# Rotating images by 90 degrees: stores no longer held until the loads have landed, and a last load in half rows

## The chip, the cores and the metric

The kernel runs on one core of one Trainium2 chip. The metric is device time in microseconds (us) of that core; lower is better. Several executions are timed without a profile, and one more is profiled.

## The reference

```python
batch, c, h, w = 32, 3, 256, 256
x = np.random.randn(batch, c, h, w).astype(np.float32)
out = np.rot90(x, k=-1, axes=(-2, -1)).astype(np.float32)
```

Each of 96 images of 256 by 256 float32 values is turned clockwise by 90 degrees: `out[b, c, i, j] = x[b, c, 255 - j, i]`. No arithmetic is done. 25.17 MB are read and 25.17 MB written.

## The kernel before

All 96 images fit into SBUF at once. They are taken as five groups `u0` to `u4` of 2, 2, 2, 4 and 2 slabs (`sizes`, line 38); a slab is 2 MB, 16 KB in each of 128 partitions. A group has a tile of its own, which is loaded, turned in place and stored, so no buffer is used twice.

**Loads.** All loads are issued by the sync engine (SP), in program order. Group 0 comes by two transfers of 1 MB (line 55) and one of 2 MB (line 56), in pieces of 8 KB. For the other groups there are as many transfers as slabs (line 66), of 2 MB each, and each writes every second partition, or every fourth in group 3 (`to[i::I]`): groups 1, 2 and 4 in pieces of 16 KB over 64 partitions, group 3 in pieces of 32 KB over 32 partitions. The very last 2 MB, slab 1 of group 4, are split in two: line 63 loads the first half `a = 0` of the group's images and line 64 the second half `a = 1`, 1 MB each, 64 pieces of 16 KB. There are fourteen loads.

**Turning.** VectorE (DVE) transposes blocks of 32 by 32. Group 0 is done by `turn_slab` (line 72), the others by `turn_group`: one quarter (or two instructions for group 3) goes into a held tile, `extra` or the PSUM tiles `spare` (line 88), the other three are turned inside the group's tile (line 93), and then ScalarE (ACT) copies the held quarter into its place (lines 78 and 98). VectorE and ScalarE follow program order, group after group.

**Stores.** Ten stores (lines 106 and 113) are issued by the sync engine as well, after all loads in program order: two for each group, each from every second partition, in pieces of 16 KB over 64 partitions. They are 2 MB each, 4 MB for group 3. A store waits until VectorE and ScalarE have finished its group. The first store also waits until the transfer of line 63, called `mark`, has landed, by a dependency put in by hand (lines 107 to 109). Since the sync engine works through its instructions in order, this holds all later stores too.

**Semaphores.** The framework gives DMA transfers eight completion semaphores in turn. The ninth transfer therefore waits on the sync engine until the first has landed, the tenth until the second has, and so on; this is what spaces the later loads.

Of the kernel before, what the change touches and what calls it, by code (L numbers as in the profile page):

```python
# [1 line left out]

# [4 lines left out]


@with_exitstack  # L10
def kernel(
    ctx: ExitStack,
    tc: tile.TileContext,
    x: bass.AP,
    out: bass.AP,
):

    nc = tc.nc
    fp32 = mybir.dt.float32

    B, C, H, W = x.shape
    P = nc.NUM_PARTITIONS
    R = 16  # L30
    E = R * W
    hw = R // 2
    low, high = slice(0, hw), slice(hw, R)

    rows_in = x.rearrange("b c h w -> (b c h) w")
    rows_out = out.rearrange("b c h w -> (b c h) w")

    sizes = (2, 2, 2, 4, 2)
    first = [sum(sizes[:n]) for n in range(len(sizes))]
    groups = [  # L40
        ctx.enter_context(tc.tile_pool(name=f"group{n}", bufs=1)).tile([P, s, E], fp32, name=f"u{n}")
        for n, s in enumerate(sizes)
    ]
    psum = ctx.enter_context(tc.tile_pool(name="psum", bufs=1, space=bass.MemoryType.PSUM))
    spare = [psum.tile([P, E // 2], fp32, name=f"spare{h}") for h in range(2)]
    extra = ctx.enter_context(tc.tile_pool(name="extra", bufs=1)).tile([P, E // 2], fp32, name="extra")

    def rows_of(rows, n):
        return rows[first[n] * P * R : (first[n] + sizes[n]) * P * R]


    ld = rows_of(rows_in, 0).rearrange("(s i p r) w -> s i p (r w)", s=2, i=2, p=P)
    home = [groups[0][:, s].rearrange("p (i f) -> p i f", i=2) for s in range(2)]
    for i in range(2):
        nc.sync.dma_start(out=home[0][:, i], in_=ld[1, i])  # L55
    nc.sync.dma_start(out=home[1], in_=ld[0].transpose([1, 0, 2]))
    for n in range(1, len(sizes)):
        I = sizes[n]
        ld = rows_of(rows_in, n).rearrange("(a i m r) w -> i m a (r w)", a=2, i=I, m=P // I)
        to = groups[n].rearrange("p s f -> p (s f)").rearrange("p (a f) -> p a f", a=2)  # L60
        for i in range(I):
            if (n, i) == (len(sizes) - 1, I - 1):
                mark = nc.sync.dma_start(out=to[i::I, 0], in_=ld[i][:, 0])
                nc.sync.dma_start(out=to[i::I, 1], in_=ld[i][:, 1])
            else:
                nc.sync.dma_start(out=to[i::I], in_=ld[i])

    def turn_slab(src, dsts):
        s = src.rearrange("p (i r g c) -> p c r g i", i=2, r=R // 2, c=R)
        for h, d in enumerate(dsts):  # L70
            d = d.rearrange("p (c k r) -> p c r k", c=hw, r=R // 2)[:, :, ::-1, ::-1]
            nc.vector.transpose(out=d, in_=s[:, h * hw : (h + 1) * hw])  # L72

    u = groups[0]
    turn_slab(u[:, 0], spare)
    turn_slab(u[:, 1], [u[:, 0, : E // 2], u[:, 0, E // 2 :]])
    for h in range(2):
        nc.scalar.copy(out=u[:, 1, h * E // 2 : (h + 1) * E // 2], in_=spare[h])  # L78

    def turn_group(n, held):  # L80
        I = sizes[n]
        T = I // 2
        K = W // (R * T)
        u = groups[n].rearrange("p s f -> p (s f)")
        src = u.rearrange("p (a t r g c) -> p t c r g a", a=2, t=T, r=R, c=R)
        dst = u.rearrange("p (i c k t r) -> p t c r k i", i=I, c=R, k=K, t=T)[:, ::-1, :, ::-1, ::-1, :]
        for t in range(T):
            nc.vector.transpose(  # L88
                out=held[t].rearrange("p (i c k r) -> p c r k i", i=I, c=hw, k=K)[:, :, ::-1, ::-1, :],
                in_=src[:, t, low, low])  # L90
        for c, r in ((low, high), (high, high), (high, low)):
            for t in range(T):
                nc.vector.transpose(out=dst[:, t, c, r], in_=src[:, t, c, r])  # L93
        back = u.rearrange("p (i c k t r) -> p t i c k r", i=I, c=R, k=K, t=T)[:, ::-1]
        for t in range(T):
            kept = held[t].rearrange("p (i c k r) -> p i c k r", i=I, c=hw, k=K)
            for i in range(I):
                nc.scalar.copy(out=back[:, t, i, low, :, high], in_=kept[:, i])  # L98

    for n, held in enumerate(([extra], [spare[1]], spare, [extra]), 1):  # L100
        turn_group(n, held)


    st = rows_of(rows_out, 0).rearrange("(s i m r) w -> i m s (r w)", s=2, i=2, m=P // 2)
    for a in range(2):
        put = nc.sync.dma_start(out=st[a], in_=groups[0][a::2])
        if a == 0:
            tc.add_manual_dep(put.ins, mark.ins.name, mybir.DependencyInfo(
                mybir.DependencyClass.Sync, mybir.DependencyReason.SCHED_ONLY), reason="stores after loads")
    for n in range(1, len(sizes)):  # L110
        st = rows_of(rows_out, n).rearrange("(a i m r) w -> a m i (r w)", a=2, i=sizes[n], m=P // 2)
        for a in range(2):
            nc.sync.dma_start(out=st[a], in_=groups[n][a::2])


# [1 line left out]
_INS = ['x']  # L117
_OUTS = [((32, 3, 256, 256), 'float32')]


# [23 lines left out]
```

## Time and profile before

| | |
|---|---|
| median of 3 runs | 122.95 us (122.94 to 122.95) |
| the profiled execution | 122.88 us |
| its span, first to last instruction | 121.1 us |
| VectorE busy | 87.4 us, 24 instructions |
| ScalarE busy | 14.9 us, 17 instructions |
| DMA, mean over the span | 416 GB/s |
| DMA packets | 3456 (384 of them under 512 B) |
| hold of the first store on the sync engine (line 106) | 31.2 us |

The page gives the busy share of the engines in forty slices of the span, and for the DMA engines the mean over the core's sixteen. "SPq" stands for the sync engine's instruction queue: an issue there is the moment when a transfer is handed to the DMA queue, not when its bytes move. The time from an issue to the landing includes the time that the transfer stands behind others. In the view of windows, a DMA share is summed from the packets that end in a window, so that it can lie a little above 1 in a short one. GB/s counts loads and stores together.

### The profile page before, as it was taken

What the parts mean: (1) busy time and instruction counts of PE and PEld (TensorE: products, weight loads), DVE (VectorE), ACT (ScalarE), POOL (GpSimd) and SP (SyncE); (2) the same over time, 40 slices, a digit from 0 to 9 for tenths busy, and PEclk for the clock granted to TensorE, in tenths of its full rate; (3) what the DMA queues carried; (4) which work ended last, traced back from release to release, by engine and by line L of the source; (5) the groups of instructions that cost most, each with busy time, mean ns of one, the idle gap of its engine ahead of it and who ended that gap; (6) DMA issues with size and microseconds to landing.
All of it is one profiled execution on the core that took longest, in us unless ns stands there. A gap on an engine that the chain in (4) does not pass through costs nothing.

```text
span 121.1 us, 131 instructions
## 1 busy us (share of the span) xinstructions
DVE 87.4 (72%) x24; ACT 14.9 (12%) x17; POOL 0.2 (0%) x4
## 2 busy tenths in 40 slices
DVE  0039999999999999999999999999999600000000
ACT  0000400380005100060000000318000330000000
POOL 0000000000000000000000000000000000000000
DMA  2999999999989898999999999999999999999994
GB/s 89 428 428 422 452 433 433 433 433 433 520 346 520 346 520 346 428 422 411 433 433 428 433 433 428 417 417 433 428 433 433 433 433 433 433 433 433 433 422 184
DMA packets 3456, 50.33 MB, mean 416 GB/s; under 512 B 384, under 2 KB 384, under 8 KB 384
## 3 DMA queue, kind: packets, MB, share of 16 engines
q1 hardware_dynamic: 3456, 50.33, 97.6%
HBM read 25.17 MB, written 25.17 MB: 416 GB/s over the span
## 4 chain that ended last, share of the span: by engine, by line
DVE 66%; issue 6%; DMA 6%; ACT 1%; ACTq 1%; SPq 0%; DVEq 0%
DVE u L93 39%; DVE spare L88 9%; DVE extra L88 6%; DVE u L72 6%; DVE spare L72 6%; DMA u<-in_x_dram 6%; ACT u L98 1%; ACTq L139 1%; SPq L55 0%; DVEq L88 0%; DVEq L72 0%
## 5 line engine op out<-in xcount | busy, mean ns | idle before, releaser
L93 DVE STREAM_TRANSPOSE u<-u 128x2048 f32<-128x2048 f32 x15 | 54.4, 3649 | 0.4
L72 DVE STREAM_TRANSPOSE spare<-u 128x2048 f32<-128x2048 f32 x2 | 7.1, 3586 | 8.1 <-DMA u<-in_x_dram 8.1
L98 ACT COPY u<-spare 128x512 f32<-128x512 f32 (+1 forms) x10 | 6.0, 687 | 38.5 <-DVE u L93 38.5
L88 DVE STREAM_TRANSPOSE spare<-u 128x2048 f32<-128x2048 f32 x3 | 10.7, 3588 | 0.0
L72 DVE STREAM_TRANSPOSE u<-u 128x2048 f32<-128x2048 f32 x2 | 7.8, 3988 | 0.0
L88 DVE STREAM_TRANSPOSE extra<-u 128x2048 f32<-128x2048 f32 x2 | 7.8, 3896 | 0.0
L98 ACT COPY u<-extra 128x1024 f32<-128x1024 f32 x4 | 4.0, 1043 | 22.8 <-DVE u L93 22.8
L78 ACT COPY u<-spare 128x2048 f32<-128x2048 f32 x2 | 3.6, 1870 | 8.7 <-DVE u L72 8.7
L78 ACT ACT_TABLE_LOAD x1 | 1.3, 1283 | 13.0 <-DMA u<-in_x_dram 13.0
L128 POOL MEMSET const-uint8-127<- 128x1 uint8 x1 | 0.1, 103 | 0.0
L128 POOL MEMSET const-bfloat16-1.0<- 128x1 bf16 x1 | 0.1, 102 | 0.0
L128 POOL MEMSET const-float32-0.0<- 128x1 f32 x1 | 0.1, 99 | 0.2 <-issue 0.2
L128 POOL MEMSET const-float32-1.0<- 128x1 f32 x1 | 0.1, 99 | 0.0
## 6 DMA issues: line engine op xcount, KB each, us to landing
u<-in_x_dram SPq DMA_DIRECT2D x10, 2048.0 KB, 30.4
out_dram<-u SPq DMA_DIRECT2D x8, 2048.0 KB, 18.2
out_dram<-u SPq DMA_DIRECT2D x2, 4096.0 KB, 21.1
u<-in_x_dram SPq DMA_DIRECT2D x4, 1024.0 KB, 20.5
```

The costliest lines, as they stand in the source:

```text
L72: nc.vector.transpose(out=d, in_=s[:, h * hw : (h + 1) * hw])
L78: nc.scalar.copy(out=u[:, 1, h * E // 2 : (h + 1) * E // 2], in_=spare[h])
L88: nc.vector.transpose(out=held[t].rearrange("p (i c k r) -> p c r k i", i=I, c=hw, k=K)[:, :, ::-1, ::-1, :], in_=src[:, t, low, low])
L93: nc.vector.transpose(out=dst[:, t, c, r], in_=src[:, t, c, r])
L98: nc.scalar.copy(out=back[:, t, i, low, :, high], in_=kept[:, i])
L128: nc = _bacc.Bacc("TRN2", target_bir_lowering=False, num_devices=1)
L139: with _tile.TileContext(nc) as tc:
```

## The change

The dependency of the first store on the transfer `mark` goes, so a store waits only for its own group (and for the turn of its semaphore). The last 2 MB are still loaded by two transfers of 1 MB, but cut in another way: each now brings one half `f` of every row of 16 KB, for both halves `a` of the group, so 128 pieces of 8 KB over the same 64 partitions two apart. Line numbers after line 109 move up by three.

```diff
             if (n, i) == (len(sizes) - 1, I - 1):
-                mark = nc.sync.dma_start(out=to[i::I, 0], in_=ld[i][:, 0])
-                nc.sync.dma_start(out=to[i::I, 1], in_=ld[i][:, 1])
+                for f in (slice(0, E // 2), slice(E // 2, E)):
+                    nc.sync.dma_start(out=to[i::I, :, f], in_=ld[i][:, :, f])
             else:
                 nc.sync.dma_start(out=to[i::I], in_=ld[i])
...
     for a in range(2):
-        put = nc.sync.dma_start(out=st[a], in_=groups[0][a::2])
-        if a == 0:
-            tc.add_manual_dep(put.ins, mark.ins.name, mybir.DependencyInfo(
-                mybir.DependencyClass.Sync, mybir.DependencyReason.SCHED_ONLY), reason="stores after loads")
+        nc.sync.dma_start(out=st[a], in_=groups[0][a::2])
```

## The prediction

> **What bounds the kernel now.** I began with the page: busy shares, the forty slices, the queues.
>
> ```profile
> DVE 87.4 (72%) x24; ACT 14.9 (12%) x17; POOL 0.2 (0%) x4
> ...
> DMA  2999999999989898999999999999999999999994
> ...
> q1 hardware_dynamic: 3456, 50.33, 97.6%
> ```
>
> VectorE works 87.4 us of 121.1. The DMA engines are full from the first slice to the last, and all 50.33 MB of loads and stores pass through one queue, q1. The chain of waits ends on VectorE and ScalarE at about 97 us, because it does not follow the last stores; I read it only as the order in which groups become ready. What sets the end is that queue. The question is therefore whether the transfers ever stand still, above all where loads end and stores begin. Next I read the timeline of the sync engine's issues, in the stretches 7 to 9, 12 to 14, 15 to 35 and around 59 us (start, duration, line, count):
>
> ```profile
> 7.98 0.60 SPq L66 DMA_DIRECT2D u<-in_x_dram  x1
> ...
> 12.95 0.60 SPq L66 DMA_DIRECT2D u<-in_x_dram  x1
> ...
> 17.84 0.61 SPq L66 DMA_DIRECT2D u<-in_x_dram  x1
> 22.75 0.51 SPq L63 DMA_DIRECT2D u<-in_x_dram  x1
> 27.64 0.49 SPq L64 DMA_DIRECT2D u<-in_x_dram  x1
> ...
> 59.43 1.37 SPq L106 DMA_DIRECT2D out_dram<-u  x2
> 60.92 39.06 SPq L113 DMA_DIRECT2D out_dram<-u  x8
> ```
>
> Each of the first five waits for an earlier load to land, so these starts are landings: the second transfer of group 0 at 7.98, its third (2 MB) at 12.95, then both of group 1 and the first of group 2. Loads land in the order of issue, one 2 MB after the other. The last load (L64) is in the queue from 27.64 on. The first store goes in at 59.43, and the view of the sync engine's waits says what it stood for:
>
> ```profile
> SPq L106 <- DMA u<-in_x_dram: 31.2, 1, 31.2
> ```
>
> That 31.2 us is the hold which the change removes. It looks large, so I asked for the windows around it, one for each 0.61 us (start and end, length, VectorE, ScalarE and GpSimd busy, clock, DMA share, GB/s):
>
> ```profile
> 59.84:60.45 0.61, 0.61 (x1) 0.00 (x0) 0.00 (x0) 1.00 1.01 430
> 60.45:61.06 0.61, 0.61 (x1) 0.00 (x0) 0.00 (x0) 1.00 1.01 430
> 61.06:61.67 0.61, 0.61 (x1) 0.00 (x0) 0.00 (x0) 1.00 1.01 430
> 61.67:62.28 0.61, 0.61 (x1) 0.00 (x0) 0.00 (x0) 1.00 1.00 430
> ```
>
> The transfers pass from loads to stores at 430 GB/s without a dip. The hold is a wait of the sync engine, not of the DMA engines.
>
> **The hold.** Removed: one semaphore wait of the first store, on L63's landing. The order of the sync engine's instructions in the changed kernel is otherwise the same: fourteen loads first, ten stores after, no load behind a store. What the first store then waits for is ScalarE's last copy of group 0 (23.03 + 3.63 = 26.7 us) and the landing of an earlier transfer that used its semaphore, the second of group 2. Landings go on from 27.64 in steps of 4.9, so that is 32.5 us. The others follow: the second store at about 37.4, group 1 at 42.3 and 47.2, group 2 at 54.2 (its copies end at 52.19 + 1.93 = 54.1) and 57.1; groups 3 and 4 as before, at 84.25 and 97.94, when their copies are done. But at 32.5 us all loads are already queued, 28 us of them, and the stores stand behind. Gain: only what is lost at the seam now. L64 was issued at 27.64 and took 34.1 us to land, 61.74; the first store was issued at 59.43 and took 7.2, 66.6. The difference is 4.9 us for 2 MB, as much as one load behind another. I take 0 for the seam, and 0.1 us (the rounding of the landing times) as the most there is to gain.
>
> That the stores stay behind the loads is the row on which all rests: from 5.6 us on some eight transfers stood in one queue at once, and every landing that the trace shows came in the order of issue. The Trainium skill ("DMA: Bandwidth & Descriptors", section "Queues, rings and completion order") says that an engine takes descriptors of one ring in order, but alternates by packets between rings of different queue rows. By its first half the removal is worth nothing; by its second, with stores on another queue than the loads, it would start the sharing that I price below as a rival.
>
> **The half rows.** Before, L63 and L64 bring 64 pieces of 16 KB each, over 64 partitions two apart; after, 128 pieces of 8 KB each, over the same partitions. That is 128 pieces more, 8 more for each of 16 engines. Same bytes, same number of transfers and of issues (L63 and L64 take 0.51 and 0.49 us on the sync engine, hidden by a queue that is 30 us ahead). The nearest row is group 0's third transfer, 2 MB in 8 KB pieces: 12.95 - 7.98 = 4.97 us. 2 MB in 16 KB pieces took 17.84 - 12.95 = 4.89, 22.75 - 17.84 = 4.91 and 27.64 - 22.75 = 4.89, on average 4.90. So half rows cost 0.07 us for the last 2 MB, and since the queue never empties, all of it goes to the end. The far row is the start: the first 2 MB in such pieces land at 7.98, though the windows show bytes from 2.3 on, 5.7 us, 0.8 more than 4.90, filling of the pipe included. That is the upper bound. Below nothing I leave 0.02, the scatter of the three steps. I take 0.07, since the third transfer stands in a full queue as these do.
>
> The same page of the skill, in "Why small descriptors are slow", puts a fixed overhead of about 3 bus cycles on a packet; 8 x 3 cycles at 850 MHz would make an estimate of 0.03 us, and the sum 122.91 on the profiled execution.
>
> **What it moves.** Group 4 is complete 0.07 us later, at 61.8 instead of 61.74, but VectorE turns to it at 81.04: hidden by 19 us. Group 3, which VectorE takes up at 52.12 just after it has landed (issued at 12.95, 39.1 us to landing: 52.05), lies ahead of the changed transfers and is not touched. The engines meet the same waits. Group 3's store is issued at 84.25; the windows show the last bytes near 119.4, and groups 3 and 4 are 12.58 MB, at 4.90 us for 2.097 MB 29.4 us; so without group 3 the queue runs dry at 90.0. A store's first bytes came 1.6 us after its issue at the start (0.73 to 2.35), so it may be issued as late as 88.4: cover 4.1 us.
>
> **Sum.** Seam 0, half rows +0.07. On the profiled execution, 122.88 us (span 121.1 and 1.78 around it), that gives 122.95. The median of the runs is 122.95, 0.07 above that execution, so the forecast is 123.02: +0.06%, where about 0.2% (0.25 us) is what a measurement of this kernel can tell from no change.
>
> **Rivals.**
>
> Stores share the engines with the loads (slower). If a store issued at 32.5 us advanced beside the loads, packet for packet, group 3's loads (19.5 us of them left then) would land up to 19.5 us later, as each landing admits another store. VectorE waits for them from 52.1 on, and group 3's store comes at 84.25 + 19.5 = 103.8. All other work in the queue would end at 90.0, so the engines would idle for 19.5 - 4.1 = 15.4 us: 138.4. It decides from a delay of group 3 above 4.1 us; a single 2 MB store overtaking (4.9 us) costs 0.8, 123.8. For it speaks that VectorE has no slack at 52.12; against it, that one queue has landed everything in order. Chance 0.09.
>
> Half rows of 8 KB two apart are dearer than the contiguous 8 KB pieces of group 0 (slower). No transfer of before reads 8 KB and leaves out the next 8 KB. Toward the bound of 0.8 that gives 123.2 to 123.75. Against it: loads of 16 KB pieces one MB apart and 32 KB pieces keep the same rate. Chance 0.13.
>
> The seam hides a stall (faster). The hold releases the first store at 59.43, only 2.3 us before the loads have landed, and one engine might wait for its store although the sum over sixteen shows no dip. Early issue would return at most 0.1 by the landings, 122.92 with the half rows counted, which is no measurable change; to pass 0.2% it needs over 0.3 us (122.7), which no row shows. Chance 0.08, half of it for a real gain.
>
> The change does nothing: the hold is removed, yet the stores still start when the loads are done. That is part of my forecast.
>
> **How the numbers follow.** The forecast has 0.68, the three rivals 0.09, 0.13 and 0.08, and 0.02 are left for a gain that I do not see. Unchanged: 0.68 and half of the seam case, 0.72. Slower by over 0.2%: 0.09 + 0.13 = 0.22. Faster: the other half of the seam case and the rest, 0.06. The range goes from 122.8 (122.95, less 0.1 for the seam and 0.02 for the pieces) to 123.8 (the far bound of the half rows, and a single store that overtakes); sharing beyond one store and a real gain are left out, less than 0.15. Its likeliest part is 122.85 to 123.1.
>
> **What would show it.** Right: 3584 packets instead of 3456; stores of group 0 issued near 32.5 and 37.4 us but landing 66 us or later; L64's second transfer landing near 61.8; 430 GB/s through 61 us; VectorE still at 52.1 for group 3; the last bytes near 119.4. Wrong: a store that lands before 61 us, an idle VectorE at 52 us, or steps of the last two load landings above 2.6 us each.

## The result: 0.3% slower, and the profile after

The changed kernel takes 123.38 us (median of 6 runs, 123.25 to 123.51) where the kernel before took 122.94 beside it: a ratio of 1.0033, 95% interval 1.002 to 1.0046. That is 0.44 us, little, but clear of the scatter. The profiled execution took 123.42 us, its span 121.6.

The page's lines that were shown of before read now:

```profile
DVE 87.4 (72%) x24; ACT 14.9 (12%) x17; POOL 0.2 (0%) x4
...
DMA  3999999999979898999999999999999999999993
...
DMA packets 3584, 50.33 MB, mean 414 GB/s; under 512 B 384, under 2 KB 384, under 8 KB 384
...
q1 hardware_dynamic: 3584, 50.33, 97.5%
```

The 128 pieces more are there. VectorE and ScalarE do what they did, and the queue still looks full. The timeline of the sync engine's issues shows that the hold is gone; the stores of group 0 go in at 32.75 us and one turn later:

```profile
22.89 5.49 SPq L64 DMA_DIRECT2D u<-in_x_dram  x2
...
32.75 5.40 SPq L106 DMA_DIRECT2D out_dram<-u  x2
...
42.44 57.67 SPq L110 DMA_DIRECT2D out_dram<-u  x8
```

They did not overtake: the view of line 106 puts their landing at 67 us and later.

```profile
DMA to landing us min/median/max: 34.6/34.7/34.7
```

What happened meanwhile to the last loads stands in the view of line 64, which now holds both transfers of half rows (issued at 22.89 and 27.78):

```profile
DMA to landing us min/median/max: 34.7/35.6/36.6
```

The first landed at 22.89 + 36.6 = 59.5, the second at 27.78 + 34.7 = 62.5: 3.0 us for 1 MB. Before, the views of lines 63 and 64 read:

```profile
DMA to landing us min/median/max: 36.5/36.5/36.5
DMA to landing us min/median/max: 34.1/34.1/34.1
```

So the last 1 MB landed at 27.64 + 34.1 = 61.74, 2.5 us after the 1 MB ahead of it (22.75 + 36.5 = 59.25). The windows of the prediction, on a grid 0.01 us later, show where the 0.5 us went (last two columns: DMA share, GB/s). A piece counts there, with all its bytes and its time, in the window in which it starts, not in the one in which it ends:

```profile
59.24:59.85 0.61, 0.58 (x2) 0.00 (x0) 0.00 (x0) 1.00 1.17 430
59.85:60.46 0.61, 0.61 (x1) 0.00 (x0) 0.00 (x0) 1.00 0.88 295
60.46:61.07 0.61, 0.61 (x1) 0.00 (x0) 0.00 (x0) 1.00 0.98 363
61.07:61.68 0.61, 0.61 (x1) 0.00 (x0) 0.00 (x0) 1.00 0.89 349
61.68:62.29 0.61, 0.61 (x1) 0.00 (x0) 0.00 (x0) 1.00 1.20 510
```

The seam that passed at 430 GB/s before now dips to 295. (On this grid the kernel before reads 403 at 61.07 and 457 at 61.68: one piece of 16 KB more or less makes 27 GB/s.) The share stays near 1: the engines are not idle, the pieces under way take longer. In the packet records of the trace (start, duration and size of every piece), 30 of the last pieces of the loads take up to 636 ns where 309 is the rule for 8 KB; the first of them starts at 59.5 us, 1.7 us before the first piece of a store (61.2).

The end of the run tells the other half. Windows of 0.61 us at the end, before, then after:

```profile
118.50:119.11 0.61, 0.00 (x0) 0.00 (x0) 0.00 (x0) 1.00 1.01 430
119.11:119.72 0.61, 0.00 (x0) 0.00 (x0) 0.00 (x0) 1.00 1.01 430
119.72:120.33 0.61, 0.00 (x0) 0.00 (x0) 0.00 (x0) 1.00 0.01 0
```

```profile
118.50:119.11 0.61, 0.00 (x0) 0.00 (x0) 0.00 (x0) 1.00 1.00 430
119.11:119.72 0.61, 0.00 (x0) 0.00 (x0) 0.00 (x0) 1.00 0.57 242
119.72:120.33 0.61, 0.00 (x0) 0.00 (x0) 0.00 (x0) 1.00 0.38 161
```

Before, all sixteen engines finish together: the last sixteen pieces end between 119.74 and 119.93 us in the packet records. After, only half of the bytes of the last round come in time (242 of 430) and the rest one piece later: eight of the last sixteen pieces end by 119.87, the other eight between 120.18 and 120.48. The records do not name the engine, but it looks as if the seam delayed some engines and not others, nothing evens that out, and the last engine sets the end.

### The profile page after: what moved, and what is told of

Same layout as the page of the kernel before. It is cut to its first block, busy times and chain, and to the rows that moved or that the text cites. A ratio compares the mean times of both kernels' runs of the same rounds, so it can differ in the third digit from the quotient of the medians.

```text
span 121.6 us, 130 instructions
## 1 busy us (share of the span) xinstructions
DVE 87.4 (72%) x24; ACT 14.9 (12%) x17; POOL 0.2 (0%) x4
## 2 busy tenths in 40 slices
DMA packets 3584, 50.33 MB, mean 414 GB/s; under 512 B 384, under 2 KB 384, under 8 KB 384
## 3 DMA queue, kind: packets, MB, share of 16 engines
q1 hardware_dynamic: 3584, 50.33, 97.5%
## 4 chain that ended last, share of the span: by engine, by line
DVE 66%; issue 6%; DMA 6%; ACT 1%; ACTq 1%; SPq 0%; DVEq 0%
DVE u L93 39%; DVE spare L88 9%; DVE extra L88 6%; DVE u L72 6%; DVE spare L72 6%; DMA u<-in_x_dram 6%; ACT u L98 1%; ACTq L136 1%; SPq L55 0%; DVEq L88 0%; DVEq L72 0%
## 5 line engine op out<-in xcount | busy, mean ns | idle before, releaser
L72 DVE STREAM_TRANSPOSE spare<-u 128x2048 f32<-128x2048 f32 x2 | 7.1, 3584 | 8.2 <-DMA u<-in_x_dram 8.2
## 6 DMA issues: line engine op xcount, KB each, us to landing
out_dram<-u SPq DMA_DIRECT2D x8, 2048.0 KB, 34.7
```

## Experiments

Theories on record were **S** (stores that stand directly behind the last loads slow these), **H** (half rows load slowly), **X** (only both together). Each kernel was timed beside the kernel before on the same chip (1 to 4 on one chip, 5 to 8 on a second, 9 to 11 on a third).

**1. Only the hold removed.** The last 2 MB as before.

```diff
-        put = nc.sync.dma_start(out=st[a], in_=groups[0][a::2])
-        if a == 0:
-            tc.add_manual_dep(put.ins, mark.ins.name, mybir.DependencyInfo(
-                mybir.DependencyClass.Sync, mybir.DependencyReason.SCHED_ONLY), reason="stores after loads")
+        nc.sync.dma_start(out=st[a], in_=groups[0][a::2])
```

> Only the hold is removed; the last 2 MB are loaded as before, in two transfers of 64 pieces of 16 KB. Theory S (stores that stand directly behind the last loads slow these down at the seam, whatever the pieces): the dip near 60 to 62 us stays, and with it most of the loss, 123.25 to 123.4 us. Theory H (the half rows themselves are slow to load): no dip, 430 GB/s through the seam, 122.9 to 123.0. Theory X (both are needed: 8 KB pieces with stores right behind them): no dip, 122.9 to 123.0.

Measured 123.40 us, ratio 1.0031 (1.0019 to 1.0043). The dip is there, with pieces of 16 KB:

```profile
59.85:60.46 0.61, 0.61 (x1) 0.00 (x0) 0.00 (x0) 1.00 1.19 349
60.46:61.07 0.61, 0.61 (x1) 0.00 (x0) 0.00 (x0) 1.00 0.76 242
61.07:61.68 0.61, 0.61 (x1) 0.00 (x0) 0.00 (x0) 1.00 1.13 403
```

The last 1 MB landed 2.9 us after the one ahead. The removal alone makes the whole loss.

**2. Only the half rows**, with the first store held on the first of the two.

```diff
-                mark = nc.sync.dma_start(out=to[i::I, 0], in_=ld[i][:, 0])
-                nc.sync.dma_start(out=to[i::I, 1], in_=ld[i][:, 1])
+                mark = nc.sync.dma_start(out=to[i::I, :, : E // 2], in_=ld[i][:, :, : E // 2])
+                nc.sync.dma_start(out=to[i::I, :, E // 2 :], in_=ld[i][:, :, E // 2 :])
```

> Only the half rows; the first store is still held, now until the first of the two transfers of half rows has landed. Theory H: the second transfer of half rows still takes about 3.0 us instead of 2.5, 123.3 to 123.45 us. Theory S: no dip, only the 0.07 us of the smaller pieces, 123.0. Theory X: as S, 123.0.

Measured 122.95 us, ratio 0.9999 (0.999 to 1.0007). The last 1 MB landed 2.5 us after the one ahead. Half rows cost nothing that can be measured: H falls, as X did by the dip of experiment 1.

**3. No hold, and one transfer for the last 2 MB.**

```diff
-                for f in (slice(0, E // 2), slice(E // 2, E)):
-                    nc.sync.dma_start(out=to[i::I, :, f], in_=ld[i][:, :, f])
+                nc.sync.dma_start(out=to[i::I], in_=ld[i])
```

> No hold, and the last 2 MB come by one transfer of 128 pieces of 16 KB, so there is one transfer less. Theory S: a dip at the seam as in the changed kernel, 123.25 to 123.4 us. Theories H and X: no dip, 122.9 to 123.0.

Measured 123.35 us, ratio 1.003 (1.0021 to 1.0039), with a dip to 295 GB/s at 59.24 and 322 at 60.46. How the last load is cut does not matter for this loss.

**4. The changed kernel once more.**

> The changed kernel once more, beside the others on one chip. All theories: 123.25 to 123.5 us, and again a dip near 60 to 62 us, the second transfer of half rows landing about 3.0 us after the first. If the dip is elsewhere or missing, it was an accident of one execution and the loss has another place.

Measured 123.38 us, ratio 1.0031 (1.0019 to 1.0042), dip to 228 GB/s at 60.46, last transfer 2.9 us. The dip belongs to the kernel.

S stood. Next came what in "standing behind" does it: **P**, that a store is in the queue at all while the last pieces are fetched, or **Q**, that it has stood there long, or that six have gathered.

**5. Hold until only the last 2 MB are missing.**

```diff
-                mark = nc.sync.dma_start(out=to[i::I, 0], in_=ld[i][:, 0])
+                nc.sync.dma_start(out=to[i::I, 0], in_=ld[i][:, 0])
...
-                nc.sync.dma_start(out=to[i::I], in_=ld[i])
+                mark = nc.sync.dma_start(out=to[i::I], in_=ld[i])
```

> As before, whole rows and a hold, but the first store is held on the transfer ahead of the last 2 MB, which lands near 57 us: the stores enter the queue some 4 us before the last bytes of the loads move, where the kernel before puts them in some 2 us ahead. Theory P (a store that stands in the queue while the last pieces ahead of it are fetched slows these, however short it has stood there): a dip near 60 to 61 us, 123.3 to 123.4 us. Theory Q (it takes a long stand, or the six stores that have gathered in the changed kernel by the seam): no dip, 122.95 to 123.05.

Measured 123.08 us, ratio 1.0004 (0.9994 to 1.0014). The time is close to Q's range, but the profile is not Q's:

```profile
59.85:60.46 0.61, 0.61 (x1) 0.00 (x0) 0.00 (x0) 1.00 1.10 403
60.46:61.07 0.61, 0.61 (x1) 0.00 (x0) 0.00 (x0) 1.00 1.14 403
61.07:61.68 0.61, 0.61 (x1) 0.00 (x0) 0.00 (x0) 1.00 0.76 322
```

The dip is there, about half as deep (last 1 MB 2.7 us), with stores that entered at 57.17.

**6. All stores but one held until the loads are done.** The dependency is on the last transfer; the scheduler then puts the second store of group 0, which has none, ahead of the first.

```diff
-                mark = nc.sync.dma_start(out=to[i::I, 0], in_=ld[i][:, 0])
-                nc.sync.dma_start(out=to[i::I, 1], in_=ld[i][:, 1])
+                nc.sync.dma_start(out=to[i::I, 0], in_=ld[i][:, 0])
+                mark = nc.sync.dma_start(out=to[i::I, 1], in_=ld[i][:, 1])
```

> The hold is moved to the very last load (landing near 61.8 us) and holds all stores but one: the second of group 0 is issued first, near 32.5 us, and stands alone behind the loads; the others come at 61.9 us, while that one store is being moved. Theory P: one store is enough, dip near 60 to 61 us, 123.3 to 123.4 us. Theory Q: one store is not six; no dip if the number counts, 122.95 to 123.05, a dip if the long stand counts.

Measured 123.08 us, ratio 1.0003 (0.9993 to 1.0012). Again a dip (322 GB/s at 59.85; last 1 MB 2.8 us) without the loss in time. One store is enough for a dip; that the time did not follow means that something else was won, which I had not in any theory.

**7. Hold until only 1.5 MB are missing.**

```diff
-                mark = nc.sync.dma_start(out=to[i::I, 0], in_=ld[i][:, 0])
+                mark = nc.sync.dma_start(out=to[i::I, 0, : E // 2], in_=ld[i][:, 0, : E // 2])
+                nc.sync.dma_start(out=to[i::I, 0, E // 2 :], in_=ld[i][:, 0, E // 2 :])
                 nc.sync.dma_start(out=to[i::I, 1], in_=ld[i][:, 1])
```

> As before, but the last 2 MB come as 0.5, 0.5 and 1 MB and the first store is held on the first of these: it enters the queue near 58.2 us, about 3 us before the last bytes of the loads move. Theory P: the slow pieces start about 1.2 us before the loads end, and the store is in the queue by then, so the dip is there, 123.3 us. Theory Q: no dip, 123.0 (one transfer more, in pieces of 8 KB, costs under 0.05).

Measured 122.77 us, ratio 0.9979 (0.997 to 0.9987): faster than both kernels, which no theory said. The seam is clean, though the first store entered at 58.32:

```profile
59.85:60.46 0.61, 0.61 (x1) 0.00 (x0) 0.00 (x0) 1.00 1.01 430
60.46:61.07 0.61, 0.61 (x1) 0.00 (x0) 0.00 (x0) 1.00 1.01 430
61.07:61.68 0.61, 0.61 (x1) 0.00 (x0) 0.00 (x0) 1.00 1.02 430
```

P as I had put it falls too: the dip needs the store to enter earlier than that, unless it is the cut in three that keeps it away.

**8. Hold until only 0.5 MB are missing.**

```diff
-                mark = nc.sync.dma_start(out=to[i::I, 0], in_=ld[i][:, 0])
-                nc.sync.dma_start(out=to[i::I, 1], in_=ld[i][:, 1])
+                nc.sync.dma_start(out=to[i::I, 0], in_=ld[i][:, 0])
+                mark = nc.sync.dma_start(out=to[i::I, 1, : E // 2], in_=ld[i][:, 1, : E // 2])
+                nc.sync.dma_start(out=to[i::I, 1, E // 2 :], in_=ld[i][:, 1, E // 2 :])
```

> As before, but the last 1 MB comes in two transfers of 0.5 MB and the first store is held until only the last of them is missing: it is issued near 60.7 us. Its first bytes move about 1.2 us after the issue, 61.9, while the loads' last bytes move near 61.1: the engines stand still for some 0.8 us, 123.6 to 123.9 us, with no slow pieces ahead of the gap. Both theories say this; it bounds the hold from the other side. If it is 122.95, the engines reach a new store faster than I think.

Measured 124.20 us, ratio 1.0094 (1.0079 to 1.011). The stores enter at 60.75, and the engines stand still for a whole window:

```profile
60.46:61.07 0.61, 0.61 (x1) 0.00 (x0) 0.00 (x0) 1.00 0.97 403
61.07:61.68 0.61, 0.61 (x1) 0.00 (x0) 0.00 (x0) 1.00 0.05 14
61.68:62.29 0.61, 0.61 (x1) 0.00 (x0) 0.00 (x0) 1.00 1.01 430
```

Here the share falls with the rate: a gap, not slow pieces. The loss of 1.17 us is more than the expected 0.8 and more than that window. But the window shows only when pieces start: in the packet records the last sixteen pieces of the loads end at 61.25 on average (the last at 61.38), and the first sixteen of the stores start at 62.14 on average (the first at 62.08), so an engine stands still for 0.89 us.

This led back to the packet records. After 64 us a store piece of 16 KB lasts 611.0 ns on average in the changed kernel and in experiments 1 and 3 to 7, but 614.6 in the kernel before, 614.4 in experiment 2 and 616.9 in experiment 8, the three whose stores came last. Experiment 5 has the loads of the kernel before, cut in the same way, so the cut is not what makes the difference. An engine moves about 90 such pieces from there to the end: 90 x 3.6 ns = 0.32 us, paid by the kernel before and not by the changed one. Theory **T** put the two together: too early costs a dip at the seam, too late costs slower stores, then a gap.

**9. Hold until only 1.25 MB are missing**, between 7 and the kernel before.

```diff
-                mark = nc.sync.dma_start(out=to[i::I, 0], in_=ld[i][:, 0])
+                mark = nc.sync.dma_start(out=to[i::I, 0, : 3 * E // 4], in_=ld[i][:, 0, : 3 * E // 4])
+                nc.sync.dma_start(out=to[i::I, 0, 3 * E // 4 :], in_=ld[i][:, 0, 3 * E // 4 :])
```

> As before, but the first of the two last MB comes in pieces of 12 KB and then of 4 KB, and the first store is held on the 12 KB pieces: it is issued near 58.9 us, between the kernel before (59.4) and the hold on 1.5 MB (58.3). Theory T (the stores have to enter the queue within a window of time: some 4 us ahead of the last loads they slow these, some 2 us ahead they come so late that the engines begin their stores in step and their pieces then take 612 to 616 ns in place of 611): inside the window, no dip at the seam, 122.75 to 122.85 us; or at its late edge, 122.95. Rival (the gain of the hold on 1.5 MB comes from splitting the last loads in three): 122.75, and with the late edge excluded by that alone.

Measured 122.83 us, ratio 0.9987 (0.9977 to 0.9997), no dip, store pieces of 611.0 ns. T's window of time holds, but not its reason for the longer pieces, engines that begin their stores in step: at 64 us the sixteen pieces under way start within 0.21 us of each other in experiment 1 (611.0 ns) and within 0.28 in the kernel before (614.6 ns). The rival, that the gain comes from cutting the last loads in three, is not excluded by this run. For the length of the store pieces it falls: experiment 8 is cut in three and has 616.9 ns, experiment 5 is not and has 611.0. For the missing dip it stays.

One window can mislead where the size of the pieces changes: this run reads 322 and 349 GB/s from 57.41 to 58.63, where pieces of 12 KB give way to pieces of 4 KB, and 510 in the next window, though no piece of 12 KB takes more than 471 ns (median 465).

**10. Experiment 7 once more**, on another chip.

> The kernel with the hold on 1.5 MB once more, on whatever chip this is. If its gain is real, 0.997 to 0.999 of the time before, 122.7 to 122.85 us, no dip at the seam; if it was an accident of the chip, 122.95.

Measured 122.80 us, ratio 0.9979 (0.9971 to 0.9988). The gain is real.

**11. Two turns from loads to stores.** The changed kernel, with the stores of group 0 in the queue ahead of group 4's loads.

```diff
+    st = rows_of(rows_out, 0).rearrange("(s i m r) w -> i m s (r w)", s=2, i=2, m=P // 2)
+    for a in range(2):
+        nc.sync.dma_start(out=st[a], in_=groups[0][a::2])
+    load(len(sizes) - 1)
```

> The changed kernel, with the two stores of group 0 placed in the queue ahead of group 4's loads: the queue now turns from loads to stores twice (near 51 and 70 us), with the stores long in the queue both times, and once from stores to loads (near 61 us). Theory P/T (every turn from loads to stores that have long stood behind them slows the last pieces of the loads): two dips, 0.3 to 0.6 us each, 123.6 to 123.9 us if they add on the same engines, 123.3 to 123.4 if they fall on different ones. Theory Q, as far as it is left (only a large heap of stores is bad): the first turn, with two stores behind the loads, has a smaller dip than the second. If a turn costs nothing by itself and the loss is bound to the last loads of the run: one dip, 123.4.

Measured 123.71 us, ratio 1.0046 (1.0032 to 1.006). The first turn now falls at group 3's pieces of 32 KB:

```profile
48.61:49.22 0.61, 0.57 (x2) 0.00 (x0) 0.00 (x0) 1.00 2.41 859
49.22:49.83 0.61, 0.61 (x1) 0.00 (x0) 0.00 (x0) 1.00 0.00 0
49.83:50.44 0.61, 0.61 (x1) 0.00 (x0) 0.00 (x0) 1.00 1.35 430
50.44:51.05 0.61, 0.61 (x1) 0.00 (x0) 0.00 (x0) 1.00 1.01 322
51.05:51.66 0.61, 0.61 (x1) 0.00 (x0) 0.00 (x0) 1.00 0.33 107
51.66:52.27 0.61, 0.61 (x1) 0.00 (x0) 0.00 (x0) 1.00 0.51 215
...
66.91:67.52 0.61, 0.61 (x1) 0.00 (x0) 0.00 (x0) 1.00 0.93 390
...
71.18:71.79 0.61, 0.61 (x2) 0.00 (x0) 0.00 (x0) 1.00 0.95 390
```

These pieces last two windows each and start together, so the windows swing between 859 and 0 GB/s even ahead of the turn, and a single low one is no rate. The cost of the first turn, with two stores behind the loads, shows in other views: the last 2 MB of group 3 took 39.9 us to land instead of 39.1 (line 66 here and in the changed kernel), 0.8 us more, and VectorE waited 0.8 us for them, within the cover of 4.1 us that the prediction had worked out. In the packet records 24 pieces of 32 KB took 1.5 to 2.0 us instead of 1.2. At the second turn, with four stores behind the loads, the windows never fall below 390, and the view of line 64 reads:

```profile
DMA to landing us min/median/max: 35.3/36.4/37.5
```

The last 1 MB landed 2.7 us after the one ahead (37.58 + 35.3 against 32.72 + 37.5), 0.2 more than in the kernel before. The turn from stores to loads near 61 us stays at 430. So a turn costs at group 3 as well, and not by the number of stores: what was left of Q falls, and the loss is not bound to the last loads of the run. But the two dips of 0.3 to 0.6 us that P/T forecast came as 0.8 and 0.2, so that 123.71 lies in its range says little. The execution that was profiled, 124.06 us, was the slowest of five.

## Why the prediction was right, and which of its terms were not

The number held: 123.38 lies in the range, 0.36 above the forecast of 123.02. But the forecast was "no change", and the ratio's interval lies at or above 1.002; the sign belongs to the slower case that I gave 0.22. That the number lies inside is luck: the upper bound of 123.8 came from dear half rows and from a store that overtakes, and neither happened.

**The half rows, +0.07: too small to be seen.** Experiment 2 gives a ratio of 0.9999, between -0.12 and +0.09 us. The rival that made them dear (0.13) was wrong; so was that case's place as the likeliest way to get slower.

**The seam, 0: this is the step that failed.** I read that the stores stay behind the loads, which is right (they landed from 67 us on), and that the seam has no dip, which is right for the kernel before; from the two I concluded that the early issue can only return something, 0 to 0.1 us. I bounded the hold's removal by what the hold might cost, and not by what it might prevent: the last 1 MB landed 3.0 us after the one ahead, not 2.5, and the hold alone decides it (experiments 1 and 2). That the transfers of a queue are taken in order does not say that they leave each other alone. The Trainium skill has the sentence that I should have weighed ("DMA: Bandwidth & Descriptors", section "Two DMAs through the same engine are not ordered"): descriptors of one engine's queue start in order but are pipelined, and an engine's read and write sides are separate queues. It would fit slow pieces that begin 1.7 us before the first store moves; no run here shows the two sides apart.

**A term that I did not have: the pieces of the stores, -0.32 us.** It is a gain of the change, hidden under the larger loss. With it the sums come close. The third column is the landing of the last load less 61.74; the fourth is 90 pieces times the difference to 614.6 ns; measured is the median less that of the kernel before beside it.

| kernel | first store enters, us | last load later | store pieces | sum | measured |
|---|---|---|---|---|---|
| changed | 32.75 | +0.74 | -0.32 | +0.42 | +0.44 |
| 4, changed again | 32.64 | +0.54 | -0.32 | +0.22 | +0.39 |
| 1, no hold | 32.72 | +0.62 | -0.32 | +0.30 | +0.41 |
| 3, one load | 27.77 | +0.46 | -0.32 | +0.14 | +0.36 |
| 6, one store free | 32.70 | +0.39 | -0.32 | +0.07 | +0.05 |
| 5, hold to 2 MB | 57.17 | +0.39 | -0.32 | +0.07 | +0.05 |
| 7, hold to 1.5 MB | 58.32 | +0.09 | -0.32 | -0.23 | -0.26 |
| 10, the same | 58.31 | +0.09 | -0.32 | -0.23 | -0.23 |
| 9, hold to 1.25 MB | 58.92 | +0.08 | -0.32 | -0.24 | -0.20 |
| before, 1 MB | 59.43 | 0 | 0 | 0 | 0 |
| 2, half rows, 1 MB | 59.48 | +0.11 | -0.02 | +0.09 | -0.04 |
| 8, hold to 0.5 MB | 60.75 | +0.07 | +0.21 | +0.28, and a gap | +1.17 |

In experiment 8 the gap of 0.89 us, added to 0.28, gives the 1.17 that were measured. The other sums stand within 0.13 us of the measured differences, except two of the kernels without a hold (3 and 4), which come out 0.2 too small. Columns two to five are of one profiled execution each, the last is of medians. The execution profiled in experiment 3 was the fastest of its eleven, 123.11 us: +0.12 by itself, and its sum is +0.14. Executions also start up to 0.15 us apart: VectorE's first wait is 8.1 us before and 8.2 after.

The bytes that the packet records show as moved, set against a steady 429 GB/s, say the same without the landings. Between 58 and 62 us the queue falls behind by 0.43 to 0.49 us in the changed kernel and experiments 1, 3 and 4, by 0.22 and 0.30 in 5 and 6, and by at most 0.06 in the kernel before and in 2, 7, 9 and 10. From 64 to 118 us the kernel before loses 0.34 us against the changed one.

**The sharing rival, 138 us, was wrong in its mechanism**, as I had judged by the order of the landings. Its cover of 4.1 us took the 1.6 us from an issue to the first bytes from a load (0.73 is line 55), not from a store; a store took 1.3 us in experiment 8 (60.75 to 62.08), which makes the cover 4.4 and changes nothing. **The seam that hides a stall** was wrong for the seam, but a gain of early issue does exist, in the stores.

**What I listed to look at** did its work. As forecast came 3584 packets, stores issued near 32.5 us and landing after 66, and VectorE at group 3 at 52.3. What I had listed for "right" and did not come was 430 GB/s through 61 us (295), the last load near 61.8 (62.5) and the last bytes near 119.4 (past 119.7). Of the two last steps between landings, which were "wrong" above 2.6 us each, the first read 2.5 and the last 3.0. It pointed at the place.

**What stays open.** The runs show when the dip comes: always when the stores enter by 57.2 us, not from 58.3 on. They do not show what in an engine slows the pieces, nor why it hits some engines only, nor why stores that come late run in longer pieces. Whether the cut in three helps to keep the dip away when stores enter at 58.3 to 58.9 us was not separated: no run with the last loads in two enters its stores between 57.2 and 59.4.

## What to carry to other kernels

Where a queue is full from end to end, a wait ahead of it can still be worth its place, because it decides what stands behind the transfers that are under way: take it away in a run of its own before calling it free. When loads turn into stores in one queue, try the moment of issue as a size: here 2.9 to 3.5 us before the last load landed (experiments 9 and 7) was best, 5.0 us (experiment 5) cost a dip, 2.3 us (the kernel before) longer store pieces, and 1.1 us (experiment 8) a gap as well. And price a removed wait on both sides: what it costs, and what it may be holding off.

## What the runs showed of the hardware that I had not expected

Loads of 8 or 16 KB pieces that ran at 430 GB/s fell to 228 to 322 GB/s in their lowest window of 0.61 us when a store stood behind them in the queue early enough: pieces of 8 KB took up to 655 ns instead of 309, pieces of 16 KB up to 1179 instead of 611, and pieces of 32 KB up to 1974 instead of 1215. Stores ahead of loads showed no such dip (430 GB/s at 61 us in experiment 11), nor did loads ahead of loads (430 in the kernel before from 59.84 on). The same stores of 16 KB pieces last 611.0 ns each, or 614 to 617 ns, for 55 us on end, according to whether the first was issued by 58.9 us or from 59.4 us on.
